# gMLP's v by seven products of halves instead of eight; the half-sums of its weight on GpSimd

## The chip, the cores and the metric

One core of a Trainium2 chip runs the whole program in one launch. The metric is the time of one execution on the device, in microseconds (us). A core has five engines that each work through an instruction list of their own, in order: TensorE (PE in the rows; its weight loads are PEld), VectorE (DVE), ScalarE (ACT), GpSimd (POOL) and SyncE (SP), whose list here issues nearly all transfers between DRAM and the on-chip memory. They wait for each other through semaphores.

## The reference

Batch 1, 512 tokens, width 1024, float32. A first block mixes three branches, then come a feed-forward part and a second block of two layers. What matters here, for h = rms_norm(x):

```
u, v, q, kv, nsa_g, xr, rg, mg = split(h @ w_in)
y_a = gelu(u) * (W_s @ layer_norm(gelu(v)) + b_s)     # gMLP: 4 chunks of 128 tokens, W_s lower triangular
y_b = nsa(q, kv, nsa_g, ...)                          # one of its parts: compress keys and values,
                                                      #   gelu((blocks + pe) @ w1) @ w2
y_c = rglru(xr, rg, ...)                              # the recurrent branch
merged = g0*(y_a @ w_br_a) + g1*(y_b @ w_br_b) + g2*(y_c @ w_br_c),   g = sigmoid(mg)
x = x + rms_norm(merged @ w_o); then the feed-forward part
```

v is 512 x 1024: h (512 x 1024) times w_v (1024 x 1024).

## The kernel before, in words

Numbers are held as two parts of lower precision, hi and lo (`split`, L140 to L150: ScalarE copies hi at L144, VectorE subtracts for lo at L145), and a product is three matmuls, hi*hi, hi*lo and lo*hi. A weight tile of 128x1024 is loaded raw by SP into `wr`, then split into `wh` and `wl` (`load_w`, L188). h lies on chip as `hT`, transposed, in both parts.

The program is written as Python generators that a clock of estimated times interleaves (`spawn`; `yield t` means "go on t us of matmul time later"); a scheduler then sets each engine's order from that and from priorities, where `load_w` is moved ahead. What results is a fixed list for each engine.

- Early, NSA's keys and values: `fold` (L1408 to L1413) copies a projection through SP into windows (`K2<-R`), `blocks` adds the position code (L1434), and the hidden layer of 16 weight tiles (nsa_wk1, then nsa_wv1, four raw tiles of 512 KB each) is followed by a gelu (L434 to L438), transposes of its result g on TensorE (L138) and the second layer. Between these, TensorE does products that are wanted later (`mgproj`, weight w_mg, L1384). The raw weights have two buffers here.
- Then the rest of NSA, the recurrent branch, and `br_b` for NSA's output.
- `gmlp` (L760): v by `T_` twice (L769 to L786), once for each half of v's columns: 96 matmuls of 128x512 each, tokens by columns. Each 128-token result goes through a gelu (ScalarE L434, L435, L437; VectorE L436, L438), its statistics (L777), and after the second half through the normalization (mean and variance L780, a small Newton iteration L154 to L166, L782). Then for each of 8 column blocks: u's block by `F_` and its gelu; `mixed` (L791), spawned with a delay of 12 for the first block and 4 for the others, which multiplies wT with all four normalized tiles vg; and `br_add` (L626 to L636), 24 matmuls with w_br_c, after which VectorE updates bT (L635) and the merged sum (L636).
- In the second block one product is already done by seven products: `TS_` computes the four quarter blocks of a product from seven products of half size, 24 matmuls each, with the weight's four half-sums taken from DRAM. `weight_sums` makes these: for a group it loads four 128x512 pieces q of the weight (L372), GpSimd subtracts four times in place (L375 to L378), SP stores four results (L381). Each of four q buffers exists once, so the next group's loads wait for the stores of the group before.

Of the kernel before, what the change touches and what calls it, by code (L numbers as in the profile page):

```python
# [7 lines left out]
F32 = mybir.dt.float32  # L8
# [3 lines left out]
ALU = mybir.AluOpType  # L12
# [38 lines left out]
class Block:  # L51
# [136 lines left out]
    def load_w(self, src, into=None):  # L188
        with self.tc.high_priority(offset=50):
            self.nr += 1  # L190
            rp, n = (self.rawp, 4) if self.rawp and self.nr % 3 else (self.wp, 2)
            raw = rp.tile([P, 1024], F32, tag="wr", name=self.nm("wr"), bufs=n)
            self.nc.sync.dma_start(out=raw, in_=src)
            if into is not None:
                self.split(*into, raw)
                return into
            self.nw += 1
            wp, n = (self.wx, 1) if self.wx and self.nw % 5 == 0 else (self.wp, 4)
            wh = wp.tile([P, 1024], F32R, tag="wh", name=self.nm("wh"), bufs=n)
# [278 lines left out]
    def block1(self):  # L478
        tc, nc, A = self.tc, self.nc, self.A
# [10 lines left out]
        self.nr, self.rawp = 0, None  # L490
# [49 lines left out]
        with tc.tile_pool(name="gmlp", bufs=1, side="right", reuse_waits="tile") as gp:  # L540
            ya = self.new_op(self.yp, "y", bufs=2)
            mT = self.gmlp(gp, ya, yc)
# [217 lines left out]
    def gmlp(self, gp, ya, yc):  # L760
# [12 lines left out]
        def done(half):  # L773
            def f(t, ps):
                o = slice(half * 512, half * 512 + 512)
                self.gelu(ps, gp, out=vg[t][:, o])
                v.bn_stats(st[t][:, half, :], vg[t][:, o])  # L777
                if half:
                    mv = self.sm(2)
                    v.bn_aggr(mv, st[t])  # L780
                    r = self.rsqrt(mv[:, 1:2])
                    v.tensor_scalar(vg[t], vg[t], mv[:, 0:1], r, op0=ALU.subtract, op1=ALU.mult)  # L782
            return f

        for half in range(2):
            self.T_(self.tok(self.hT), A["w_v"][half], 8, done(half), outer=2 + 2 * half)  # L786

        ps = self.pst()
# [32 lines left out]
    def ffn(self, hf, fp, es_w):  # L821
# [5 lines left out]
        def done(i, ps):  # L827
            if i == 0:
# [5 lines left out]
                self.w_sums = {}  # L834
# [535 lines left out]
    def nsa(self):  # L1370
# [27 lines left out]
        with tc.tile_pool(name="cmp", bufs=1, side="right", reuse_waits="tile") as cp:  # L1398
# [4 lines left out]
            k2s = []  # L1403

# [367 lines left out]
```

## Time and profile before

| | |
|---|---|
| median of three runs | 2508.74 us (2506.1 to 2509.05) |
| the profiled execution | 2508.13 us, its span 2506.3 us |
| busy: PE, DVE, ACT, POOL | 2483.5, 1469.9, 1081.4, 179.0 us |
| TensorE's granted clock, mean | 0.999 of full speed |
| chain of work that ended last, by engine | PE 89%, DVE 4%, ACT 3%, DMA 2% |
| TensorE's largest waits in the whole span | 2.7 us for wl (five times), 2.2 us for the first gain row |

The span is what the trace covers; the time lies 1.83 us above it. The profile's page gives the busy time of each engine and follows the chain of work back from the last instruction. A row of a timeline is start, duration, engine, line, operation, result<-operands; in brackets stands the idle time before it and what ended it. TensorE's matmuls overlap: one of 128x512 has a duration of 0.39 us, but starts come closer together.

### The profile page before, as it was taken

To read this page: it belongs to the slowest core of one execution; us is meant where nothing else is said; L and a number is where in the kernel's file an instruction comes from. 1 tells how busy PE (TensorE), PEld (TensorE's weight loads), DVE (VectorE), ACT (ScalarE), POOL (GpSimd) and SP (SyncE) were. 2 spreads that over 40 slices of the span, in tenths; PEclk is the share of its full clock that TensorE was granted. 3 is DMA by queue.
4 is the path that set the end of the run, shared out by engine and by line. 5 is a ranking of instruction groups with operands and counts; after the bars stand their busy time and mean duration, and the time that the engine had idled before them with its cause. 6 is when DMAs were issued, how large, how long until landed. Compare 5 with 4: busy or idle time off the path is not lost.

```text
span 2506.3 us, 31435 instructions
## 1 busy us (share of the span) xinstructions
PE 2483.5 (99%) x11802; PEld 2047.5 (82%) x11802; DVE 1469.9 (59%) x2719; ACT 1081.4 (43%) x1852; POOL 179.0 (7%) x152
## 2 busy tenths in 40 slices
PE   9999999999999999999999999999999999999998
PEld 7877777888888888888888788888888888888887
DVE  6567665776656787626633536765484343375635
ACT  4477666875334333324443532333253344223323
POOL 0023332000000110001100000003020000000000
PEclk9999999999999999999999999999999999999999
DMA  6522222223345886544432222226454222322233
GB/s 183 173 79 78 72 70 93 93 91 110 118 130 173 269 273 211 183 139 141 165 119 92 63 87 82 91 78 219 147 171 154 90 84 63 98 76 93 68 101 118
DMA packets 110074, 309.54 MB, mean 124 GB/s; under 512 B 14409, under 2 KB 20425, under 8 KB 109794
## 3 DMA queue, kind: packets, MB, share of 16 engines
q1 hardware_dynamic: 109200, 306.29, 38.1%
q8 instruction: 92, 1.51, 0.3%
q10 hardware_dynamic: 722, 1.25, 0.1%
q14 instruction: 60, 0.49, 0.1%
HBM read 273.84 MB, written 21.00 MB: 118 GB/s over the span
## 4 chain that ended last, share of the span: by engine, by line
PE 89%; DVE 4%; ACT 3%; DMA 2%; issue 1%; POOL 1%; SPq 0%; ACTq 0%; DVEq 0%; POOLq 0%
PE ps L129 86%; PE ps L138 3%; DVE wl L145 1%; DMA wr<-in_w_out_dram 1%; ACT S L1534 1%; ACT wh L144 1%; DMA wr<-in_w_o_dram 0%; DVE H L145 0%; DVE yr L145 0%; POOL X L1077 0%; DVE PTl L145 0%; DVE S L1528 0%; DMA wr<-in_w_v_dram 0%; POOL S L1541 0%; ACT S L1539 0%
## 5 line engine op out<-in xcount | busy, mean ns | idle before, releaser
L129 PE MATMUL ps<-h,wh 128*128 128x512 f32 (+1 forms) x4000 | 1244.4, 391 | 0.0
L129 PEld LDWEIGHTS ps<-h,wh 128*128 128x128 f32 x4000 | 734.7, 188 | 139.5 <-issue 5.1
L145 DVE TENSOR_TENSOR wl<-wr,wh 128x1024 fp32r<-128x1024 f32 x395 | 492.6, 1250 | 486.9 <-ACT wh L144 486.5
L129 PE MATMUL ps<-h,wl 128*128 128x512 f32 (+1 forms) x2000 | 774.0, 387 | 0.1
L144 ACT ACTIVATE wh<-wr 128x1024 fp32r<-128x1024 f32 x395 | 417.3, 1059 | 807.0 <-PE ps L129 627.9
L129 PEld LDWEIGHTS ps<-h,wl 128*128 128x128 f32 x2000 | 376.2, 188 | 75.4 <-DVE wl L145 0.5
L129 PE MATMUL ps<-wh,h 128*128 128x512 f32 x672 | 211.6, 392 | 0.0
L129 PEld LDWEIGHTS ps<-wh,h 128*128 128x128 f32 x672 | 126.3, 188 | 27.0 <-DVE h L145 0.8
L129 PE MATMUL ps<-wl,h 128*128 128x512 f32 x336 | 131.5, 391 | 0.9 <-DVE wl L145 0.9
L129 PE MATMUL ps<-y,wh 128*128 128x512 f32 x384 | 119.4, 391 | 0.0
L129 PE MATMUL ps<-wh,f 128*128 128x512 f32 x288 | 89.7, 390 | 0.0
L1541 POOL TENSOR_SCALAR S<-S,sm 128x128 f32<-128x128 f32 (+3 forms) x64 | 69.6, 1099 | 213.6 <-ACT Q L144 77.7
L129 PEld LDWEIGHTS ps<-y,wh 128*128 128x128 f32 x384 | 71.5, 188 | 14.3
L375 POOL TENSOR_TENSOR q<-q,q 128x512 f32<-128x512 f32 x8 | 11.8, 1474 | 950.9 <-DMA q<-in_w_va_dram 950.9
L129 PE MATMUL ps<-yr,wh 128*128 128x512 f32 x256 | 78.8, 389 | 0.0
L660 DVE SCALAR_TENSOR_TENSOR acc<-aw,cact,acc 128x512 f32<-128x512 f32 x96 | 75.7, 790 | 5.1 <-issue 2.3
L1534 ACT ACTIVATE S<-S,sm 128x128 f32<-128x128 f32 (+3 forms) x128 | 70.2, 550 | 19.1 <-DVE sm L1532 18.8
L145 DVE TENSOR_TENSOR PTl<-ps,PTh 128x512 fp32r<-128x512 f32 (+1 forms) x96 | 65.1, 684 | 22.5 <-ACT PTh L144 21.6
L144 ACT ACTIVATE PTh<-ps 128x512 fp32r<-128x512 f32 (+1 forms) x96 | 56.0, 588 | 49.1 <-PE ps L138 43.9
L1131 DVE CUSTOM_DVE_ANT_0 P<-ps,c_masks 128x128 f32<-128x128 f32 (+1 forms) x96 | 31.2, 325 | 76.3 <-PE ps L129 74.1
L129 PEld LDWEIGHTS ps<-wl,h 128*128 128x128 f32 x336 | 63.2, 188 | 14.5 <-DVE wl L145 1.9
L129 PE MATMUL ps<-y,wl 128*128 128x512 f32 x192 | 74.8, 390 | 0.0
(362 smaller groups left out, 3331.7 us busy)
## 6 DMA issues: line engine op xcount, KB each, us to landing
aw<-in_w_ada_dram SPq DMA_DIRECT2D x96, 256.0 KB, 4.3
wr<-in_w_qk_dram SPq DMA_DIRECT2D x48, 512.0 KB, 3.5
wr<-in_w_ffn_in_dram SPq DMA_DIRECT2D x44, 512.0 KB, 3.9
wr<-in_w_g_dram SPq DMA_DIRECT2D x32, 512.0 KB, 3.5
wr<-in_w_qr_dram SPq DMA_DIRECT2D x32, 512.0 KB, 3.4
wr<-in_w_mg_dram SPq DMA_DIRECT2D x24, 512.0 KB, 3.5
wr<-in_w_ffn_out_dram SPq DMA_DIRECT2D x22, 512.0 KB, 3.9
wr<-in_w_va_dram SPq DMA_DIRECT2D x20, 512.0 KB, 5.6
```

What stands on the lines that cost most here:

```text
L129: self.nc.tensor.matmul(out, a, b, start=start, stop=stop, skip_group_check=True)
L138: self.nc.tensor.transpose(out, in_, self.ident[:k, :k])
L144: nc.scalar.activation(hi, src, AF.Copy)
L145: nc.vector.tensor_sub(lo, src, hi.bitcast(F32))
L375: g.tensor_sub(b11, b12, b11)
L660: v.scalar_tensor_tensor(acc, w, self.cact[:, k:k + 1], acc, op0=ALU.mult, op1=ALU.add)
L1131: v.tensor_tensor_reduce(dst, pv, mask, 1.0, -3e38, ALU.add, ALU.max, mx[:, n:n + 1])
L1534: nc.scalar.activation(Ps[h], Ps[h], AF.Exp, scale=0.125, bias=nm_[:, h:h + 1], accum_out=ls[:, h:h + 1])
L1541: nc.gpsimd.tensor_scalar(Ps[h], Ps[h], r[:, h:h + 1], None, op0=ALU.mult)
```

## The change

v is computed by `TS_`: seven products of 24 matmuls in place of two `T_` of 96. Four half-sums of h are made first, in the four vg tiles: two additions on VectorE, two on GpSimd (L790), then three operations on VectorE (L791 to L794) and one on GpSimd (L795); they are split into a tile hs. Two results are kept in e (in `yt` buffers), others in the upper halves of vg; VectorE adds products up from PSUM (L345 to L361). The weight's half-sums come from DRAM (`w_sums["v", 0]`), where `weight_sums` puts them: it is spawned in NSA's compressed branch with paces 3.0, 6.5 and 2.5 and a delay of 6.0, and its q tiles lie in that branch's pool. During `TS_` two of four raw weight tiles go to the pool wx, and its wh and wl are not used for split weights. ya takes its buffer after `TS_`.

```diff
 load_w:
-            rp, n = (self.rawp, 4) if self.rawp and self.nr % 3 else (self.wp, 2)
+            rp, n, tag = (self.rawp, 4, "wr") if self.rawp and self.nr % 3 else (self.wp, 2, "wr")
+            if self.raws_in_wx and self.nr % 4 > 1:
+                rp, n, tag = self.wx, 1, "wh" if self.nr % 4 == 2 else "wl"
...
-            wp, n = (self.wx, 1) if self.wx and self.nw % 5 == 0 else (self.wp, 4)
+            wp, n = (self.wx, 1) if self.wx and not self.raws_in_wx and self.nw % 5 == 0 else (self.wp, 4)
 gmlp:
-        for half in range(2):
-            self.T_(self.tok(self.hT), A["w_v"][half], 8, done(half), outer=2 + 2 * half)
+        hs = self.new_op(self.yp, "y", bufs=2)
+        flat = lambda x, j: x[:, 2 * j:2 * j + 2, :].rearrange("p k q -> p (k q)")
+        a12, a21, a11, a22 = vg
+        for x, kh, th in ((a21, 0, 1), (a22, 1, 1), (a11, 0, 0), (a12, 1, 0)):
+            part = (slice(None), slice(4 * kh, 4 * kh + 4), slice(256 * th, 256 * th + 256))
+            (v if th else nc.gpsimd).tensor_add(x.rearrange("p (k q) -> p k q", k=4), self.hT.hi[part].bitcast(F32),
+                                                self.hT.lo[part].bitcast(F32))
+        v.tensor_add(a22, a21, a22)
+        v.tensor_sub(a21, a11, a21)
+        v.tensor_sub(a11, a22, a11)
+        nc.gpsimd.tensor_sub(a12, a12, a11)
+        for j, x in ((1, a11), (0, a22), (2, a21), (3, a12)):
+            self.split(flat(hs.hi, j), flat(hs.lo, j), x)
+        places = iter([gp.tile([P, S], F32, tag="yt", name=self.nm("e"), bufs=2) for _ in range(2)]
+                      + [vg[t][:, 512:] for t in range(4)])
+        self.raws_in_wx = True
+        self.TS_(self.hT, [A["w_v"][i] for i in range(2)], self.w_sums["v", 0],
+                 lambda j, k, t, lo: flat(hs.lo if lo else hs.hi, j)[:, k * 256 + t * P:k * 256 + t * P + P],
+                 lambda: next(places), done)
+        self.raws_in_wx = False
+        ya = self.new_op(self.yp, "y", bufs=2)
 nsa, compressed branch:
+            self.w_sums["v", 0] = self.dp.tile([8, P, D], F32, tag="v0", name="v0")
+            self.spawn(self.weight_sums([A["w_v"][i] for i in range(2)], self.w_sums["v", 0], cp, (3.0, 6.5, 2.5)), 6.0)
```

How the orders change, at the two places of which the prediction speaks. In the names a number behind a tile tells its use apart; lines after L372 are 1 to 20 higher in the changed program.

**The SP queue in the compressed branch.** Before, from the last load of nsa_wk1 on (wr are raw weights of 512 KB):

```order
L193 DMA wr_691<-in_nsa_wk_dram 128x1024
L193 DMA wr_733<-in_w_mg_dram 128x1024
L193 DMA wr_771<-in_nsa_wv_dram 128x1024
L193 DMA wr_794<-in_nsa_wv_dram 128x1024
L193 DMA wr_812<-in_nsa_wv_dram 128x1024
L193 DMA wr_830<-in_nsa_wv_dram 128x1024
L193 DMA wr_857<-in_w_mg_dram 128x1024
L193 DMA wr_913<-in_w_k_dram 128x1024
```

The changed order in the same place, from the load of w_mg on (q are the pieces of w_v that GpSimd works on, v_388 is the DRAM tile of its half-sums):

```order
L195 DMA wr_778<-in_w_mg_dram 128x1024
L195 DMA wr_820<-in_nsa_wv_dram 128x1024
L383 DMA v_388<-q_682 128x512
L383 DMA v_388<-q_686 128x512
L383 DMA v_388<-q_684 128x512
L383 DMA v_388<-q_688 128x512
L195 DMA wr_843<-in_nsa_wv_dram 128x1024
```

and six rows further on:

```order
L374 DMA q_864<-in_w_v_dram 128x512
L195 DMA wr_887<-in_nsa_wv_dram 128x1024
L383 DMA v_388<-q_858 128x512
L383 DMA v_388<-q_862 128x512
L383 DMA v_388<-q_860 128x512
L195 DMA wr_914<-in_w_mg_dram 128x1024
L383 DMA v_388<-q_864 128x512
L195 DMA wr_978<-in_w_k_dram 128x1024
```

The second load of nsa_wv1 has moved behind the four stores of one group, the next w_mg load behind three stores of the next.

**TensorE and VectorE at the first use of v.** TensorE before, the end of w_br_c's second product (ps_6373) with the first matmuls of wT and the normalized tiles vg between its own:

```order
L129 MATMUL ps_6373<-y_4644,wh_6369 128x512
L129 MATMUL ps_6373<-y_4645,wh_6369 128x512
L129 MATMUL ps_6373<-y_4644,wl_6370 128x512
L129 MATMUL ps_6383<-wT,vg_5844 128x128
L129 MATMUL ps_6383<-wT,vg_5845 128x128
L129 MATMUL ps_6383<-wT,vg_5846 128x128
L129 MATMUL ps_6383<-wT,vg_5847 128x128
L129 MATMUL ps_6373<-y_4644,wh_6369 128x512
L129 MATMUL ps_6373<-y_4645,wh_6369 128x512
```

TensorE in the changed order, the end of w_br_c's second product (ps_6486):

```order
L129 MATMUL ps_6486<-y_4709,wh_6482 128x512
L129 MATMUL ps_6486<-y_4710,wh_6482 128x512
L129 MATMUL ps_6486<-y_4709,wl_6483 128x512
L129 MATMUL ps_6496<-wT,vg_5907 128x128
L129 MATMUL ps_6514<-wT,vg_5907 128x128
L129 MATMUL ps_6543<-h_96,wh_6539 128x512
L129 MATMUL ps_6543<-h_97,wh_6539 128x512
L129 MATMUL ps_6543<-h_96,wl_6540 128x512
L129 MATMUL ps_6543<-h_96,wh_6539 128x512
```

VectorE in the changed order, from bT's update with ps_6486 on:

```order
L636 SCALAR_TENSOR_TENSOR bT_6478<-bT_6478,ps_6486 128x512
L162 SCALAR_TENSOR_TENSOR sm_6310<-sm_6307,sm_6304 128x1
L777 BN_STATS bn_5912<-vg_5908 128x6
L166 SCALAR_TENSOR_TENSOR sm_6311<-sm_6310,sm_6307 128x1
L637 TENSOR_TENSOR mg_777<-mg_777,bT_6478 128x512
L162 SCALAR_TENSOR_TENSOR sm_6314<-sm_6311,sm_6304 128x1
L780 BN_AGGR sm_6338<-bn_5912 128x2
L438 SCALAR_TENSOR_TENSOR g_6397<-g_6397,g_6396 128x512
L166 SCALAR_TENSOR_TENSOR sm_6315<-sm_6314,sm_6311 128x1
L145 TENSOR_TENSOR wl_6712<-wr_6709,wh_6711 128x1024
```

and on to the normalization (L782) of the tile vg_5907 that TensorE's next matmul wants:

```order
L162 SCALAR_TENSOR_TENSOR sm_6318<-sm_6315,sm_6304 128x1
L440 SCALAR_TENSOR_TENSOR g_6398<-g_6397,g_6396 128x512
L166 SCALAR_TENSOR_TENSOR sm_6319<-sm_6318,sm_6315 128x1
L154 TENSOR_SCALAR sm_6340<-sm_6338 128x1
L782 TENSOR_SCALAR vg_5907<-vg_5907,sm_6302,sm_6319 128x1024
```

Before, VectorE had v's four normalizations done ahead of that update; now the last two stand behind it, and the first matmul with wT has moved from between the next product's matmuls to right behind w_br_c's last.

## Rows read from the trace of the kernel before

**Rows 1.** The page's part 1: busy us, share of the span, instructions.
```profile
PE 2483.5 (99%) x11802; PEld 2047.5 (82%) x11802; DVE 1469.9 (59%) x2719; ACT 1081.4 (43%) x1852; POOL 179.0 (7%) x152
```

**Rows 2.** Windows: stretch, us, then busy time by engine; clock, DMA share, GB/s.
```profile
36.00:100.00 64.00, 62.19 (x332) 52.37 (x331) 36.17 (x43) 30.01 (x40) 0.25 (x2) 1.00 0.62 180
...
585.00:640.00 55.00, 55.00 (x243) 45.19 (x242) 39.83 (x84) 27.34 (x40) 0.00 (x0) 1.00 0.31 100
```

**Rows 3.** Timeline of PE from 583.9 us: start, us, operation (x2: two matmuls).
```profile
584.01 0.62 PE L129 MATMUL ps<-wh,h 128*128 128x512 f32 x2
...
584.69 0.62 PE L129 MATMUL ps<-wh,h 128*128 128x512 f32 x2
```

**Rows 4.** Tile q (weight sums of the second block): its transfers, both ways.
```profile
DMA to landing us min/median/max: 2.2/3.8/5.9
```

**Rows 5.** DMA issues, 815 to 1740 us: count, KB each, median us to landing.
```profile
va<-q SPq DMA_DIRECT2D x32, 256.0 KB, 3.8
...
wr<-in_w_va_dram SPq DMA_DIRECT2D x10, 512.0 KB, 6.2
```

**Rows 6.** Timeline of POOL, one group of four subtractions: start, us.
```profile
1718.96 1.29 POOL L375 TENSOR_TENSOR q<-q,q 128x512 f32<-128x512 f32 x1 [5.91 <-DMA q<-in_w_va_dram]
1720.33 2.15 POOL L376 TENSOR_TENSOR q<-q,q 128x512 f32<-128x512 f32 x1
...
1723.93 1.30 POOL L378 TENSOR_TENSOR q<-q,q 128x512 f32<-128x512 f32 x1
```

**Rows 7.** Timeline of the SP queue's issues, 60 to 90 us (x4: from first to last).
```profile
60.44 2.39 SPq L1413 DMA_DIRECT2D K<-R  x4
...
66.63 0.33 SPq L193 DMA_DIRECT2D wr<-in_w_mg_dram  x1
71.16 10.99 SPq L193 DMA_DIRECT2D wr<-in_nsa_wv_dram  x4
82.97 0.33 SPq L193 DMA_DIRECT2D wr<-in_w_mg_dram  x1
```

**Rows 8.** Timeline of ACT, 74 to 88 us: start, us, [idle before <- what ended it].
```profile
74.60 1.06 ACT L144 ACTIVATE wh<-wr 128x1024 fp32r<-128x1024 f32 x1 [3.06 <-DMA wr<-in_nsa_wv_dram]
...
77.90 0.41 ACT L437 ACTIVATE g<-g 128x256 f32<-128x256 f32 x1
...
87.42 1.06 ACT L144 ACTIVATE wh<-wr 128x1024 fp32r<-128x1024 f32 x1 [1.06 <-DMA wr<-in_w_mg_dram]
```

**Rows 9.** Timeline of PE, 80 to 90 us.
```profile
80.72 0.44 PE L138 MATMUL ps<-ident,g 128*128 128x128 f32 x2 [0.50 <-DVE g L438]
...
89.10 0.63 PE L129 MATMUL ps<-h,wh 128*128 128x512 f32 x2
```

**Rows 10.** Timelines of PE and DVE where T_ for gMLP's v begins.
```profile
578.80 0.39 PE L129 MATMUL ps<-wh,h 128*128 128x512 f32 x1
...
579.33 0.69 DVE L145 TENSOR_TENSOR y<-xc,y 128x512 fp32r<-128x512 f32 x1 [0.70 <-ACT y L144]
```

**Rows 11.** Timeline of DVE from 619 us: operations that follow each other without idle time.
```profile
619.22 0.68 DVE L436 SCALAR_TENSOR_TENSOR g<-g,g 128x512 f32<-128x512 f32 x1
619.83 1.22 DVE L145 TENSOR_TENSOR wl<-wr,wh 128x1024 fp32r<-128x1024 f32 x1
620.96 0.68 DVE L438 SCALAR_TENSOR_TENSOR vg<-g,g 128x512 f32<-128x512 f32 x1
```

**Rows 12.** Timeline of DVE, 1713 to 1720 us: the same split with POOL idle, then busy.
```profile
1713.54 1.23 DVE L145 TENSOR_TENSOR wl<-wr,wh 128x1024 fp32r<-128x1024 f32 x1 [1.64 <-ACT wh L144]
1718.97 2.36 DVE L145 TENSOR_TENSOR wl<-wr,wh 128x1024 fp32r<-128x1024 f32 x1 [4.21 <-ACT wh L144]
```

**Rows 13.** Timelines of DVE and PE: v's last normalization, its first use.
```profile
634.03 0.16 DVE L166 SCALAR_TENSOR_TENSOR sm<-sm,sm 128x1 f32<-128x1 f32 x1
634.23 0.81 DVE L782 TENSOR_SCALAR vg<-vg,sm,sm 128x1024 f32<-128x1024 f32 x1
...
641.58 1.05 PE L129 MATMUL ps<-wT,vg 128*128 128x128 f32 x8
```

More of the change, by code (lines that the diff above doesn't have):

```diff
@@ L190, in load_w @@
             self.nr += 1
-            rp, n = (self.rawp, 4) if self.rawp and self.nr % 3 else (self.wp, 2)
-            raw = rp.tile([P, 1024], F32, tag="wr", name=self.nm("wr"), bufs=n)
+            rp, n, tag = (self.rawp, 4, "wr") if self.rawp and self.nr % 3 else (self.wp, 2, "wr")
+            if self.raws_in_wx and self.nr % 4 > 1:
+                rp, n, tag = self.wx, 1, "wh" if self.nr % 4 == 2 else "wl"
+            raw = rp.tile([P, 1024], F32, tag=tag, name=self.nm("wr"), bufs=n)
             self.nc.sync.dma_start(out=raw, in_=src)
@@ L489, in block1 @@
         self.nw, self.wx = 0, None
-        self.nr, self.rawp = 0, None
+        self.nr, self.rawp, self.raws_in_wx, self.w_sums = 0, None, False, {}
         self.wp = op(self.es, "w")
@@ L540, in block1 @@
         with tc.tile_pool(name="gmlp", bufs=1, side="right", reuse_waits="tile") as gp:
-            ya = self.new_op(self.yp, "y", bufs=2)
-            mT = self.gmlp(gp, ya, yc)
+            mT = self.gmlp(gp, yc)
         es_m.close()
@@ L757, in rnn, with gmlp @@
         fill()
-    def gmlp(self, gp, ya, yc):
+    def gmlp(self, gp, yc):
         nc, A, v = self.nc, self.A, self.nc.vector
@@ L771, in gmlp @@
         st = [self.smp.tile([P, 2, 6], F32, tag="bn", name=self.nm("bn"), bufs=6) for _ in range(4)]
[L773 to L783, printed above, removed]
@@ L785, in gmlp, with done @@
-        for half in range(2):
-            self.T_(self.tok(self.hT), A["w_v"][half], 8, done(half), outer=2 + 2 * half)
+        def done(t, half, z):
+            o = slice(half * 512, half * 512 + 512)
+            self.gelu(z, gp, out=vg[t][:, o])
+            v.bn_stats(st[t][:, half, :], vg[t][:, o])
+            if half:
+                mv = self.sm(2)
+                v.bn_aggr(mv, st[t])
+                r = self.rsqrt(mv[:, 1:2])
+                v.tensor_scalar(vg[t], vg[t], mv[:, 0:1], r, op0=ALU.subtract, op1=ALU.mult)
@@ L833, in done @@
                 self.spawn(self.ada(pool[0], 1.2))
-                self.w_sums = {}
                 self.spawn(self.all_weight_sums(0, pool[0], (12.0, 16.0, 12.0)))
```

## The prediction, made before the changed kernel was run

> **What bounds the kernel now.** The page's first part comes first: TensorE (PE) is busy 99% of the span, VectorE (DVE) 59%, GpSimd (POOL) 7% [rows 1]. So an instruction off TensorE costs time only where TensorE waits for it, and a matmul that goes is worth its pitch. The windows of the two stretches the change touches say the same: from 585 to 640 us, where gMLP's v is computed, TensorE never stops, and from 36 to 100 us, the stretch of NSA's compressed branch, it stands for 1.8 us [rows 2]. I then read both programs' orders, queue by queue, looked for the rows on which TensorE waits in the changed one, and priced them from the rows below. Every engine and the SP queue (which issues the loads) works in order: what stands behind a waiting row waits too.
>
> The sum is made on the profiled execution, 2508.13 us. The median of the three runs, 2508.74 us, lies 0.6 us above it, which is less than anything said here. About 5 us (0.2%) is what a measurement of this kernel can tell from no change: the bounds are 2503.7 and 2513.8.
>
> **The change, part by part.**
>
> *24 matmuls less.* Two T_ of 96 become seven products of 24: 192 to 168. Three matmuls of 128x512 take from 584.01 to 584.69, 0.227 us each [rows 3]. 24 x 0.227 = **-5.45 us**, all of it on the path.
>
> *The weight's sums beside the compressed branch.* They add 32 transfers of 256 KB on the SP queue, among the loads that feed TensorE there, and 16 GpSimd subtractions. GpSimd did almost nothing in this stretch, so only the SP queue matters. Of the four groups the first two lie where SP stood still anyway (nothing of them is on the path). The last two I follow with the rows of the same code for the second block: a 256 KB load lands after 3.8 us [rows 4], a store after 3.8 us [rows 5], and the four subtractions take from 1718.96 to 1725.23, 6.3 us [rows 6].
> - The last K<-R copies are issued from 60.44 to 62.83 [rows 7]. Group 2's last stores follow them, some 0.4 us each, to about 63.8. Group 3's loads write the buffers those stores read, so the last waits till 63.8 + 3.8 = 67.6, and lands at 71.4. The subtractions start when the first two are there (about 70.5): the fourth ends at 76.8.
> - The four stores of group 3 now stand before the second load of wv. It is issued at about 77.2 and lands after 3.4 us (as the first one, issued at 71.16 and used at 74.60 [rows 7, 8]) to 6.2 us (a load beside much traffic [rows 5]): 80.6 to 83.4. On ScalarE its split (1.06) stands ahead of the gelu's tanh, which was done at 77.90 [rows 8]; then come the tanh (0.41) and 0.4 on VectorE, and TensorE's transposes of g start at 82.5 to 85.3, not at 80.72 [rows 9].
> - Group 4's loads wait for group 3's stores to land (77.2 + 3.8 = 81.0) and land at 84.8; the subtractions run from about 83.5. The next mg load stands behind the stores of the first three, so it is issued at about 88.8 instead of 82.97. Before, 4.45 us passed from that issue to its split at 87.42, and 1.68 from there to TensorE's first use at 89.10 [rows 7 to 9]. 88.8 + 4.45 + 1.68 = 94.9: **+5.8 us**. With a landing of 3.4 or 6.2 us it is 4.8 or 7.6. This holds the 1.8 to 4.6 us of the step before, since TensorE then only waits less here. Nothing gives it back: TensorE's order holds no other work there. The least is 0, if every landing is much quicker.
>
> One page of the Trainium skill would make this cheaper: "DMA: Bandwidth & Descriptors" (Anatomy of one DMA — SWDGE (gpsimd) path) fits 2.0 us plus bytes/436e3 for transfers that GpSimd issues, an estimated 2.6 us for 256 KB. The rows have 3.8 on SP's queue [rows 4, 5]. By the page the chain's four transfers would be 4.8 us shorter, this term about 1 us and the sum 2513.9. I go by the rows.
>
> *The opening of the seven products.* The half-sums of h need VectorE just when the first weights need their low parts (wl). VectorE is done with the recurrent branch at 579.33 + 0.61, TensorE begins at 578.80 [rows 10]. A 128x1024 operation holds VectorE for 1.13 us, a 128x512 one for 0.61 us [rows 11]. Ahead of the wl of the third product's second weights stand ten of the first and two of the second kind, 12.5 us; it ends at 593.6 and is wanted after 61 matmuls, at 592.65: 1.0 late. Of the next product's weights the first wl stands two splits further on, ends at 597.0 and is wanted after 73 matmuls, at 595.4: 1.6 late in all. The second of those splits waits for GpSimd's 128x1024 subtraction, which follows VectorE's at 591.3 and takes 2.6 to 4.3 us (twice its 128x512 rows, 1.29 in [rows 6] and up to 2.15 beside VectorE): with 1.06 on ScalarE and two operations on VectorE the wl ends at 597.2 to 598.9, up to 3.5 late. While GpSimd worked on two tensors, a wl took 2.36 us instead of 1.23 [rows 12]; of VectorE's operations here three lie beside GpSimd's, 3.4 us more at most. So 1.6 to 6.9; I take **+3.0**, nearer the low end, since GpSimd's two additions can start before VectorE's.
>
> The rule behind that last row is in "GPSIMD Engine Reference" (Specifications) of the Trainium skill: GpSimd shares its SBUF interfaces with VectorE, against instructions with two SBUF inputs. The trace agrees, with 2.36 us against 1.23. If the rule held for all 128x1024 operations here, the term would be 6.9 and the sum 2522.6.
>
> *The layer norm of v comes too late.* The largest term. Before, the last normalization of v (634.23 + 0.81) was done 6.5 us before TensorE's first matmul on it (641.58) [rows 13]. Seven products finish v's tiles nearly together at their end, and VectorE has some dozen more additions from PSUM and six more wl before it. In the changed order TensorE's very next row after the last matmul of w_br_c's second product is the matmul of wT with vg; on VectorE, bT's update, which waits for that last matmul, stands 14 rows ahead of the normalization of that vg. So whatever VectorE did before, TensorE stands while VectorE does five 128x512 operations (3.0 us), a wl (1.13), eight small ones (some 0.1 each; 0.16 alone) and the normalization (0.81) [rows 11, 13]: 5.8 us. Six matmuls later the next vg is wanted, and VectorE needs 3.2 us for it (two 128x512, eight small ones, 0.81) while TensorE has 1.8 us of work: 1.4 more. **+7.2 us**. The low end is 5.8; if VectorE comes to bT up to 2.3 us behind TensorE it is 9.5. It should be nearly level there: from the sixth product's first result VectorE has 27 operations of 128x512, seven wl, two normalizations and some 26 small ones up to bT, 29 us; TensorE has 127 matmuls, 28.8 us.
>
> *No cost.* The third and later splits of half-sums on ScalarE lie in its idle time; six more 512 KB loads at 0.33 us of SP each are covered, since SP is mostly idle beyond 100 us; w_sums' reads replace reads of w_v. If that cover fails it is a wl late by a landing, 3.4 us once.
>
> **Sum:** 2508.13 - 5.45 + 5.8 + 3.0 + 7.2 = **2518.7 us**.
>
> **The rivals.**
> 1. *Only the products count* (faster). The sums hide in SP's idle time and the normalization is done before TensorE asks. Then 2508.13 - 5.45 = 2502.7. For it: GpSimd and SP have much idle time. Against: the order of VectorE's rows around bT, which no duration can undo. It decides at TensorE's first wT matmul: this case needs it to start within 0.5 us of w_br_c's last.
> 2. *The compressed branch hides the sums, the rest is as forecast.* 2518.7 - 5.8 = 2512.9: not measurably slower, or just. Its condition is that each of the chain's four transfers is 1.4 us shorter than 3.8; the shortest of this kind took 2.2 [rows 4]. This is where the skill's page on DMA, above, would put it.
> 3. *Everything at its upper end*: 2508.13 - 5.45 + 7.6 + 6.9 + 9.5 = 2526.7. This is where GpSimd slows VectorE on every row they share and loads are slow beside the sums' traffic.
> 4. *The change does less than it says*: seven products that start late for want of weights, as half the raw loads go to other buffers. TensorE's order has 24 rows less, so the products are there; the first raw tile's buffer comes free 50 matmuls (11.4 us) ahead, where a landing of 3.4 and a split of 2.2 are needed. Only a landing beside heavy traffic, twice, would cost: 2518.7 + 2 x (6.2 - 3.4) = 2524.3.
>
> **How the numbers follow.** The forecast has 0.52, rival 1 0.05, rival 2 0.22, rival 3 0.14, rival 4 0.07. The range goes from 2507, which takes in rival 2 with the low ends of its terms (2508.13 - 5.45 + 0 + 0 + 5.8 = 2508.5), to 2530, above rivals 3 and 4. Faster has rival 1 and a little more: 0.06. Of rival 2, and of the forecast with low ends, 0.18 lies below 2513.8: same. Slower 0.76.
>
> **What would show it.** In the changed profile TensorE's list of waits has a new wait on VectorE's normalization (about 6 and then 1 us), waits on wl near the third and fourth product, and after 80 us longer waits for the transposes' g or the next mg's wl; the window from 36 to 100 us holds some 6 us less TensorE work. TensorE has 24 matmuls fewer. I am wrong if the wT matmul follows w_br_c's without a gap, or if the mg load is issued before 85 us.

## The result, and the profile after

The changed kernel takes **2530.75 us** (median of five runs, 2526.8 to 2533.52), the kernel before 2508.74 on the same chip: ratio 1.009, 95% interval 1.0079 to 1.0101, slower by 22 us. The forecast was 2518.7 in a range of 2507 to 2530: the sign is right, the size is half of what came, and the range ends 0.75 us too low. The profiled execution took 2533.52 us, the slowest of the five; its span is 2531.7.

TensorE has the 24 matmuls less, and VectorE, ScalarE and GpSimd have more to do (the page's part 1; before: [rows 1]):

```profile
PE 2490.3 (98%) x11778; PEld 2050.7 (81%) x11778; DVE 1499.4 (59%) x2746; ACT 1092.7 (43%) x1864; POOL 210.9 (8%) x171
```

Fewer matmuls with more busy time is the first hint: the matmuls themselves became slower. I cut the span at three instructions that both programs have: the first matmul of K with Q, at 121.58 us before; the first matmul for gMLP's v, at 578.80; and the first of the feed-forward part, at 808.42. That makes four stretches: NSA's compressed branch, attention and recurrent branch, gMLP, and the rest. After, they are 13.3, 0.2, 9.5 and 2.4 us longer, although gMLP holds 24 matmuls less. So both losses lie where the change works. The rest differs by -1.8 to +2.4 us between kernels that are the same there; the 2.4 of this execution hold two waits for a weight, 0.81 and 0.76 us at 2495.80 and 2497.06, and a granted clock of 0.50 from 2498 to 2500, which no other kernel has there. TensorE's waits in the whole span (line, what it waited for: total us, times, longest):

```profile
PE ps L129 <- DVE wl L145: 9.3, 10, 3.9
PE ps L129 <- DVE sm L156: 7.0, 1, 7.0
PE ps L129 <- ACT wh L144: 3.9, 3, 1.7
PE ps L138 <- DVE g L440: 3.0, 1, 3.0
```

Before, wl was waited for 2.7 us in all, and the other three together under 2 us. The windows (columns as in [rows 2], the first and third stretch answer to its rows) show what the waits did besides:

```profile
36.00:100.00 64.00, 55.74 (x276) 46.64 (x274) 36.71 (x39) 24.31 (x32) 18.10 (x14) 0.95 0.81 255
92.00:94.00 2.00, 2.00 (x11) 2.00 (x11) 1.69 (x2) 0.56 (x2) 1.92 (x2) 0.50 0.48 182
585.00:640.00 55.00, 51.14 (x216) 41.34 (x215) 48.46 (x56) 32.58 (x41) 5.52 (x1) 0.97 0.47 152
612.00:614.00 2.00, 1.06 (x3) 0.92 (x4) 2.00 (x3) 2.00 (x4) 0.00 (x0) 0.82 0.10 18
614.00:616.00 2.00, 2.00 (x6) 1.54 (x6) 2.00 (x4) 1.79 (x3) 0.00 (x0) 0.50 0.97 287
616.00:618.00 2.00, 2.00 (x9) 1.62 (x8) 1.49 (x2) 1.03 (x2) 0.00 (x0) 0.83 0.75 250
668.00:670.00 2.00, 2.00 (x8) 1.45 (x7) 1.26 (x4) 0.00 (x0) 0.00 (x0) 0.50 0.00 0
```

The seventh number is the clock granted to TensorE. It was 1.00 in both stretches before. Now, behind each longer wait, it is 0.50 for some microseconds: the lower of its two levels, 1.2 instead of 2.4 GHz. TensorE's timeline behind the wait in the opening of the seven products shows the price; compare the pitch with [rows 3]:

```profile
608.69 0.39 PE L129 MATMUL ps<-wh,y 128*128 128x512 f32 x1
612.93 0.53 PE L129 MATMUL ps<-wl,y 128*128 128x512 f32 x1 [3.86 <-DVE wl L145]
613.28 1.04 PE L129 MATMUL ps<-wh,y 128*128 128x512 f32 x2
614.11 0.63 PE L129 MATMUL ps<-wl,y 128*128 128x512 f32 x1
...
615.82 1.03 PE L129 MATMUL ps<-wh,y 128*128 128x512 f32 x2
616.67 0.41 PE L129 MATMUL ps<-wl,y 128*128 128x512 f32 x1
```

The eight matmuls from 613.28 to 616.67 take 3.39 us, 0.42 each; at 0.227 it would be 1.82. The wait of 3.86 us cost 1.6 us more than its length.

**The compressed branch.** The SP queue (before: [rows 7]):

```profile
68.50 2.70 SPq L374 DMA_DIRECT2D q<-in_w_v_dram  x4
71.26 0.42 SPq L195 DMA_DIRECT2D wr<-in_w_mg_dram  x1
75.70 0.33 SPq L195 DMA_DIRECT2D wr<-in_nsa_wv_dram  x1
76.85 5.24 SPq L383 DMA_DIRECT2D v<-q  x4
82.20 0.38 SPq L195 DMA_DIRECT2D wr<-in_nsa_wv_dram  x1
...
90.17 3.57 SPq L383 DMA_DIRECT2D v<-q  x3
94.02 0.33 SPq L195 DMA_DIRECT2D wr<-in_w_mg_dram  x1
```

The second load of wv stands behind four stores, and goes out at 82.20, the mg load at 94.02 instead of 82.97. An earlier mg load is late too: it stands behind the third group's loads and goes out at 71.26 instead of 66.63. TensorE pays (its rows with more than 1 us of idle time from 36 us to this stretch's end; before: [rows 9]):

```profile
78.69 0.73 PE L129 MATMUL ps<-h,wh 128*128 128x512 f32 x2 [1.39 <-ACT wh L144]
80.66 0.69 PE L129 MATMUL ps<-h,wl 128*128 128x512 f32 x1 [1.24 <-DVE wl L145]
90.48 0.44 PE L138 MATMUL ps<-ident,g 128*128 128x128 f32 x2 [2.95 <-DVE g L440]
100.32 0.73 PE L129 MATMUL ps<-h,wh 128*128 128x512 f32 x2 [1.69 <-ACT wh L144]
```

The first two are the product with the weight of that earlier mg load. ScalarE's split of it stood until the load landed (ScalarE's timeline):

```profile
77.58 1.06 ACT L144 ACTIVATE wh<-wr 128x1024 fp32r<-128x1024 f32 x1 [2.68 <-DMA wr<-in_w_mg_dram]
```

**The normalization of v.** VectorE, then TensorE (before: [rows 13]); the third block is before's TensorE row behind the eight matmuls of wT in those rows:

```profile
660.11 0.68 DVE L636 SCALAR_TENSOR_TENSOR bT<-bT,ps 128x512 f32<-128x512 f32 x1
...
665.03 0.81 DVE L782 TENSOR_SCALAR vg<-vg,sm,sm 128x1024 f32<-128x1024 f32 x1
```

```profile
665.99 1.20 PE L129 MATMUL ps<-wT,vg 128*128 128x128 f32 x4 [6.99 <-DVE sm L156]
666.84 1.20 PE L129 MATMUL ps<-h,wh 128*128 128x512 f32 x2
...
669.55 2.35 PE L129 MATMUL ps<-wT,vg 128*128 128x128 f32 x12
671.65 0.72 PE L129 MATMUL ps<-h,wh 128*128 128x512 f32 x2
```

```profile
642.38 0.71 PE L129 MATMUL ps<-y,wh 128*128 128x512 f32 x2
```

It is the row that the forecast named: bT's update 14 rows ahead of the normalization, TensorE idle over all of them, and for 1.1 us before, since VectorE came to the update that much behind TensorE's last matmul.

### The profile page after: what moved, and what is told of

Its sections match the earlier page's. It is cut to its first block, busy times and chain, and to the rows that moved or that the text cites. A ratio compares the mean times of both kernels' runs of the same rounds, so it can differ in the third digit from the quotient of the medians.

```text
span 2531.7 us, 31526 instructions
## 1 busy us (share of the span) xinstructions
PE 2490.3 (98%) x11778; PEld 2050.7 (81%) x11778; DVE 1499.4 (59%) x2746; ACT 1092.7 (43%) x1864; POOL 210.9 (8%) x171
## 4 chain that ended last, share of the span: by engine, by line
PE 85%; DVE 6%; ACT 3%; DMA 3%; issue 1%; POOL 1%; SPq 0%; ACTq 0%; POOLq 0%; DVEq 0%
PE ps L129 82%; PE ps L138 3%; DVE wl L145 2%; DMA wr<-in_w_out_dram 1%; ACT S L1554 1%; ACT wh L144 1%; DMA wr<-in_w_o_dram 0%; DMA wr<-in_w_mg_dram 0%; DVE H L145 0%; SPq L1433 0%; DVE yr L145 0%; DVE PTl L145 0%; DVE S L1548 0%; DVE xc L712 0%; DVE lr L689 0%
## 5 line engine op out<-in xcount | busy, mean ns | idle before, releaser
L145 DVE TENSOR_TENSOR wl<-wr,wh 128x1024 fp32r<-128x1024 f32 x401 | 501.5, 1254 | 485.2 <-ACT wh L144 484.6
L144 ACT ACTIVATE wh<-wr 128x1024 fp32r<-128x1024 f32 x401 | 423.2, 1058 | 805.3 <-PE ps L129 610.7
L129 PE MATMUL ps<-wh,h 128*128 128x512 f32 x592 | 187.7, 394 | 0.3 <-ACT h L144 0.3
L129 PEld LDWEIGHTS ps<-wh,h 128*128 128x128 f32 x592 | 111.6, 189 | 24.3 <-DVE h L145 0.8
L129 PE MATMUL ps<-wl,h 128*128 128x512 f32 x296 | 116.1, 392 | 0.9 <-DVE wl L145 0.9
L377 POOL TENSOR_TENSOR q<-q,q 128x512 f32<-128x512 f32 x12 | 18.1, 1512 | 863.7 <-DVE sm L164 485.1
L129 PEld LDWEIGHTS ps<-wl,h 128*128 128x128 f32 x296 | 56.0, 189 | 13.3 <-DVE wl L145 2.0
```

The source lines that it names most:

```text
L129: self.nc.tensor.matmul(out, a, b, start=start, stop=stop, skip_group_check=True)
L144: nc.scalar.activation(hi, src, AF.Copy)
L145: nc.vector.tensor_sub(lo, src, hi.bitcast(F32))
L377: g.tensor_sub(b11, b12, b11)
```

## The experiments

The theory after the result: the forecast's three waits are there and of about the forecast's size; the rest is TensorE's clock behind them. If so, each wait that is cured gives back more than its length. The rivals: the traffic of the sums slows everything, or VectorE's and GpSimd's added work does. The first kernels undo one part each, the later ones look for a place where the sums cost nothing. All results first; the last four columns are the four stretches defined above, against before's, in us, from each profiled execution.

| kernel | median us | ratio, 95% interval | compressed | attention, recurrent | gMLP | rest |
|---|---|---|---|---|---|---|
| the change | 2530.75 | 1.0090, 1.0079 to 1.0101 | +13.3 | +0.2 | +9.5 | +2.4 |
| e1 sums only | 2520.38 | 1.0049, 1.0036 to 1.0061 | +13.9 | 0.0 | -0.6 | -0.5 |
| e2 sums in recurrent branch | 2538.48 | 1.0122, 1.0108 to 1.0136 | +0.6 | +14.6 | +7.3 | +7.3 |
| e3 a split later | 2529.31 | 1.0084, 1.0070 to 1.0097 | +17.7 | +0.1 | +5.0 | -1.8 |
| e4 first use of v later | 2525.23 | 1.0071, 1.0057 to 1.0085 | +15.4 | 0.0 | +0.9 | 0.0 |
| e5 GpSimd's queue | 2530.39 | 1.0089, 1.0075 to 1.0103 | +13.3 | +0.2 | +11.9 | +0.4 |
| e6 a half-sum on VectorE | 2527.04 | 1.0079, 1.0065 to 1.0093 | +12.7 | +0.1 | +6.6 | -0.5 |
| e7 e4, e5 and e6 | 2519.64 | 1.0051, 1.0038 to 1.0063 | +11.7 | -0.4 | -1.5 | +0.9 |
| e8 sums in attention | 2529.97 | 1.0085, 1.0071 to 1.0099 | +0.5 | +11.1 | +8.6 | +0.8 |
| e9 transfers alone | 2513.09 | 1.0017, 1.0008 to 1.0026 | +7.9 | -0.1 | -0.9 | +0.5 |
| e10 e8, e4, splits later | 2519.52 | 1.0040, 1.0028 to 1.0053 | +0.8 | +11.5 | -3.5 | +0.3 |
| e11 sums 60 us later | 2514.86 | 1.0026, 1.0016 to 1.0035 | +0.8 | +8.2 | -2.4 | +0.6 |
| e12 fourth group at 423 us | 2505.94 | 0.9990, 0.9981 to 0.9999 | +1.1 | -0.2 | -2.4 | +0.9 |
| e13 fourth group at 343 us | **2506.19** | 0.9993, 0.9984 to 1.0002 | +1.1 | +1.1 | **-2.5** | -1.5 |

The stretches are of one execution each. The code of the compressed branch is the same in the change, e3, e4 and e6, and shows +12.7 to +17.7; that of gMLP is the same in the change, e5 and e8, and shows +8.6 to +11.9. By its time, the theory of the run came true in e1, e6, e12 and e13, the rival in e3, e5, e7, e8, e10 and e11; e2 is slower than both had it, e4 and e9 lie between. The stretches say which part of each theory failed.

**e1: the sums without the seven products** (before's kernel, with the change's line in the compressed branch).

```diff
+            self.w_sums["v", 0] = self.dp.tile([8, P, D], F32, tag="v0", name="v0")
+            self.spawn(self.weight_sums([A["w_v"][i] for i in range(2)], self.w_sums["v", 0], cp, (3.0, 6.5, 2.5)), 6.0)
```

> The kernel before (v by two T_, 192 matmuls) with the weight's half-sums made in the compressed branch and read by nothing. Theory (loads behind the sums' stores on the SP queue stop TensorE there, whatever is done with the sums): TensorE's transposes of g near 90.5 us as in the changed kernel and 13 us in all, 2508.7 + 13 = about 2522. Rival (the sums hide, the loss belongs to gMLP): about 2509, transposes near 81 us.

12 us slower with not one matmul less. The losses of the change split cleanly: 13 to 14 us belong to the sums in their place, the 9.5 to gMLP.

**e9: the same without GpSimd's subtractions.** The sums of the second block's second layer lose theirs too, which is outside the stretch.

```diff
-                g.tensor_sub(b11, b12, b11)
...
+                if pace[0] > 10:
+                    g.tensor_sub(b11, b12, b11)
...
```

> The kernel before with the sums' 32 transfers in the compressed branch, but without GpSimd's subtractions (the pieces are copied from w_v to DRAM, and nothing reads them). Same traffic as with the sums alone (2520.4, 12.5 us above the kernel before), no stores that wait for GpSimd. Theory (it is the chain load, 6.3 us of subtractions, store, load in front of the weights): two groups' subtractions, 12 us, leave the chain, and at most 4 us are lost, 2512 or less. Rival (the 8 MB of traffic is what delays the weights): 2518 or more.

The loss falls from 13.9 to 7.9 us in that stretch, with one wait over 1 us left from 36 us on (2.35). This execution was the slowest of eleven, though: by the medians the loss falls from 12.5 to 5.2 us. So the traffic and the stores ahead of the loads make about half of it (0.42 by the medians, 0.57 by the stretches). The other half goes with GpSimd's subtractions: the time they add to the chain load, subtract, store, and what they cost VectorE beside them (in the change a wl at 78.67 took 1.94 us, before 1.2). This run doesn't separate the two.

**e5: the sums' transfers on GpSimd's queue.** GpSimd's clearing of R goes to VectorE; the second layer's second sums go to that queue as well.

```diff
+        dma = (self.nc.sync if pace[0] > 10 else g).dma_start
...
-                    self.nc.sync.dma_start(out=q[-1], in_=src[half][c][:, o])
+                    dma(out=q[-1], in_=src[half][c][:, o])
```

> The changed kernel with the sums' transfers issued by GpSimd itself instead of SP (and the small memset of fold on VectorE, so that nothing of the branch waits for GpSimd). The traffic and the subtractions are the same. Theory (the order on SP's queue is what stops the loads): w_mg and nsa_wv are issued as in the kernel before, and most of the 13.3 us up to the first K,Q matmul goes: 2530.75 - 10 = about 2520. Rival (the traffic delays the loads): less than 3 us of it goes, 2528 or more.

Not a microsecond gained: 13.3 again. Freed from the SP queue, the sums' loads start while the kernel's first weights come in, whose issues are then 3.5 and 5.3 us later, and the waits have moved forward. TensorE's largest one:

```profile
75.76 1.12 PE L138 MATMUL ps<-ident,g 128*128 128x128 f32 x4 [7.09 <-ACT g L1439]
```

The order of the queue was one way of losing the time, not the cause by itself: in either order this stretch lost 13 us to the sums and their 8 MB (16 pieces in, 16 out, 256 KB each).

**e2: the sums in the recurrent branch**, their pieces in the spare weight buffers of wx.

```diff
-            self.spawn(self.weight_sums(..., cp, (3.0, 6.5, 2.5)), 6.0)
+            self.sums_in_wx = True
+            self.spawn(self.weight_sums(..., None, (6.0, 10.0, 6.0)), 6.0)
```

> The changed kernel with the sums moved out of the compressed branch into the recurrent one (their pieces in the two tiles of the pool wx, which the split weights give up there). Theory: the 13.3 us that the changed kernel had lost when the seven products began come back, 2530.75 - 13.3 = 2517.5, transposes near 81 us; up to 2522 if the fifth weight buffer was needed. Rival (the sums cost the same wherever they stand, by traffic): about 2530.

The first stretch is whole again (+0.6), and as much is lost where the sums are now, +14.6: four waits of TensorE over 1 us sum to 9.1, and (1 - granted clock) adds up to 5.1. (The flag of the edit also keeps later split weights out of wx, to which I put the +7.3 in the rest; no run tests that.) On SP three stores wait for their subtractions with a weight of xr behind them (SP's timeline):

```profile
451.68 5.43 SPq L388 DMA_DIRECT2D v<-q  x3
457.20 0.39 SPq L195 DMA_DIRECT2D wr<-in_w_xr_dram  x1
```

TensorE's largest wait of the stretch has another cause. GpSimd's four subtractions of a group run from 479 to 487 us, and beside them three of VectorE's operations, in front of the row that TensorE wants, take 1.72 to 1.75 us; in the kernel before they take 0.68 to 0.74. That is 3.1 of the 4.61 us (TensorE; one of the three; the same one before):

```profile
486.56 1.10 PE L129 MATMUL ps<-xh,gh 128*128 128x512 f32 x2 [4.61 <-ACT xh L144]
```

```profile
482.42 1.74 DVE L758 TENSOR_TENSOR xc<-xc,g 128x512 f32<-128x512 f32 x1
```

```profile
473.08 0.68 DVE L748 TENSOR_TENSOR xc<-xc,g 128x512 f32<-128x512 f32 x1
```

So in this place the rival that GpSimd's added work slows VectorE is true in part.

**e4: the normalization ahead of its use.** `mixed` is spawned with longer delays, so that TensorE has other products to do first, and the gelu's buffers are three.

```diff
-            yield 12.0 if c == 0 else 4.0
+            yield (26.0, 18.0, 12.0, 6.0, 4.0, 4.0, 4.0, 4.0)[c]
```

> The changed kernel with the first products of wT and v put later in TensorE's order (delays 26, 18, 12 and 6 for the first four column blocks, a third buffer for u's gelu). Theory: TensorE has u's third block to do while VectorE normalizes; the wait of 7.0 us goes, and with it some 2.7 us at half clock: 2530.75 - 9.6 = about 2521. Rival (VectorE's amount of work is the bound, not the order): the wait returns at the later place, 2528 or more.

The wait of 6.99 is gone, one of 1.50 at the third product is new, and gMLP falls from +9.5 to +0.9: 8.6 us for 5.5 us of waiting. Against e8 and e5, whose gMLP is the change's, it is 7.7 us for 5.9 and 11.0 for 6.1. That more comes back than the waits' length, each time, is the theory's main evidence. The medians lie only 5.5 us apart, not the 9.6 expected: the change's profiled execution was its slowest, and e4's compressed branch lost 2.1 us more.

**e3: the fourth half-sum split after the fifth product began; e6: that half-sum on VectorE.** In e3 the split reads its tile after part of it has been overwritten, so v is another one.

```diff
e3:
-        for j, x in ((1, a11), (0, a22), (2, a21), (3, a12)):
+        for j, x in ((1, a11), (0, a22), (2, a21)):
...
+        late = lambda: self.split(flat(hs.hi, 3), flat(hs.lo, 3), a12)
e6:
-        nc.gpsimd.tensor_sub(a12, a12, a11)
+        v.tensor_sub(a12, a12, a11)
```

> The changed kernel with the split of the fourth half-sum of h (the one GpSimd makes) written after the fifth product instead of ahead of the fourth. Theory: the wl of the fourth product no longer stands behind it on VectorE; the wait of 3.9 us at 612.9 goes, and with it the 1.7 us that the matmuls after it lost at half clock: 2530.75 - 5.5 = 2525.2. Rival (VectorE is behind anyway and the same time is lost at the normalization): 2530.

> The changed kernel with the fourth half-sum of h made by VectorE instead of GpSimd (1.1 us in place of 5.5 us). Theory (that GpSimd subtraction is what the split and the wl behind it waited for): the wait at 612.9 falls from 3.9 to at most 1 us, with the half-clock stretch behind it, 2530.75 - 4.5 = about 2526. Rival (VectorE's one operation more makes it later): 2530 or more.

Both take the wait of 3.86 away. As the wait of the normalization grew, to 9.24 and 7.81, and e6 has a new one of 1.46 at the third product, each has 1.6 us of waiting less in all; gMLP gains 4.5 and 2.9 us (3.6 and 2.0 against e8, the least of the change's gMLP). Again more comes back than the length of the waits. In e3 this hardly shows in the time, since its compressed branch lost 4.4 us more than the change's.

**e7: e4, e5 and e6 together.**

> The changed kernel with the three edits together: transfers of the sums on GpSimd's queue, the fourth half-sum on VectorE, the first products of wT later. Theory (three separate causes, and what is left is 24 matmuls less): from the seven products to the end 3 to 5 us less than in the kernel before, in the compressed branch 0 to 4 us more; 2508 - 4 + 2 = 2506, no more than 2510. Rival (the causes are one lack of VectorE or DMA capacity that moves on): 2515 or more.

The time is the rival's, but not by its reason: gMLP is 1.5 us faster than before's, and what is left is the compressed branch, where the part from e5 gave 1.6 us at most.

**e8: the sums in the attention stretch**, in four mg tiles that are free there. **e10: e8 with e4 and three of the four splits later.**

```diff
+        mgs = [self.mp.tile([P, S], F32, tag="mg", name=self.nm("mg"), bufs=8) for _ in range(8)]
...
+            self.spawn(self.weight_sums(..., mgs[4:], (9.0, 12.0, 6.0)), 10.0)
```

> The changed kernel with the sums moved to NSA's attention stretch, their pieces in the four mg tiles that are not yet in use there (the eight mg tiles are allocated ahead). Theory (the sums cost where TensorE's weights come just in time, and nothing where the loads run ahead): first K,Q matmul as in the kernel before (121.6), at most 3 us lost up to the recurrent branch, 2530.75 - 13.3 + (0 to 3) = 2517 to 2521. Rival (they cost some 13 us wherever they stand, as in the recurrent branch): 2530.

> The changed kernel with the sums in the attention stretch, the first products of wT later, and three of the four splits of h's half-sums written after the third and fourth product (the tiles dealt out so that nothing is overwritten early). Theory (what is left is 24 matmuls less): 2508 - 5.45, with 0 to 3 us for the sums and at most 2 at the third product: 2503 to 2508. Rival (VectorE's additional work turns up at another wait): 2512 or more.

The loss moved once more: 11 us in attention, most of it at these two of e8's TensorE rows (6.3 us) and in the slower clock behind them (3.4). In e10 gMLP itself is now 3.5 us faster than before's.

```profile
126.18 0.44 PE L129 MATMUL ps<-K,Q 128*128 128x128 f32 x2 [2.95 <-DVE sm L1551]
146.92 1.27 PE L138 MATMUL ps<-ident,S 128*128 128x128 f32 x4 [3.39 <-POOL S L1564]
```

**e11: the sums 60 us later**, started from the list of projections; mg's last ones come after the others.

```diff
-            seq += take(2) + [(mgproj, 4), (qproj, 6), (qproj, 7)] + take(4) + [(mgproj, 5), (mgproj, 6)] + take(16)
+            seq += take(2) + [(qproj, 6), (qproj, 7)] + take(1) + [(sums, ())] + take(16) + [(mgproj, 4), (mgproj, 5), (mgproj, 6)]
```

> The changed kernel with all cures of e10_all_moved in the gMLP stretch (normalization ahead of the matmuls of wT, the splits of three half-sums later), and the sums of w_v again in the attention stretch, in the four tiles of mg that stand free there, but 60 us later: at about 178 to 212 us instead of 119 to 160, where the first K and Q copies and the first S rows of GpSimd stand in before. The last four projections of mg come after the other fillers, so that the four tiles are free. If the 11.0 us that e8_sums_in_attention and the 11.6 that e10_all_moved lost in that stretch came from the collision with the first copies and S rows, this placement loses 0 to 3 us there, the gMLP stretch keeps its 3.2 us and the sum is 2505.5 to 2508.5 (ratio 0.999 to 1.000). If GpSimd's four subtractions in a chain (5.2 us, in front of rows on which TensorE's transposes wait) or the traffic cost the same wherever they stand, it loses 8 to 12 us again and the sum is 2514 to 2518 (ratio 1.002 to 1.004).

8.2 us are lost, which is the rival's number, but at one place. Beside three of the four groups TensorE waits no longer than 0.4 us. Beside the fourth, GpSimd waited for its loads with S rows behind it (GpSimd's timeline), TensorE for those S rows (its own), and the clock fell (window):

```profile
217.92 1.27 POOL L388 TENSOR_TENSOR mg<-mg,mg 128x512 f32<-128x512 f32 x1 [5.15 <-DMA mg<-in_w_v_dram]
...
223.31 1.83 POOL L1578 TENSOR_SCALAR S<-S,sm 128x256 f32<-128x256 f32 x2
```

```profile
224.29 0.69 PE L138 MATMUL ps<-ident,S 128*128 128x128 f32 x2 [6.35 <-POOL S L1578]
```

```profile
228.00:230.00 2.00, 2.00 (x7) 1.71 (x6) 1.85 (x5) 0.00 (x0) 0.00 (x0) 0.50 0.18 47
```

**e12 and e13: the fourth group elsewhere.** In e12 other paces move it behind the last S rows; there two of mg's projections are written into the group's tiles between its loads and its subtractions, so these sums and projections come out changed. In e13 a projection of mg goes through the first tile and holds the group's load back, mg's last projections wait for the sums, and the paces are 4, 6 and 2. The other three groups' subtractions begin within 2.5 us of e11's in both.

```diff
e12:
-            (9.0, 12.0, 6.0)
+            (12.0, 16.0, 6.0)
e13:
+            T = mgs[4] if AHEAD.index(i) == 9 else np_.tile([P, S], F32, tag="ma", name=self.nm("ma"), bufs=2)
...
+                summing.append(self.spawn(self.weight_sums(..., mgs[4:], (4.0, 6.0, 2.0), groups)))
...
+ take(1) + [(sums, (0, 1, 2))] + take(9 - 5) + [(sums, (3,))] + take(16) + [(lambda: self.wait(*summing), ()), ...
```

> e11_sums_late with other paces (12, 16, 6 instead of 9, 12, 6), by which GpSimd's subtractions of the fourth group come after its last S rows, in the gap that before shows at 413 to 433 us, instead of at 217.9, where GpSimd waited 5.15 us for the group's loads with an S row behind it and TensorE then waited 6.35 us for that row. If that one in-order wait and the lower clock behind it made e11's loss in the attention stretch (9.0 us), the stretch now loses 0 to 3 us, and the sum is 2505 to 2508.5 (ratio 0.9985 to 1.0005): the first version not slower than before. If the loss is spread over the four groups and their traffic, it stays at 2512 to 2515 (ratio 1.0015 to 1.003), and a wait shows beside another group or where ScalarE writes mg behind the last stores.

> e11_sums_late with the fourth group of sums held back: one of the projections of mg that are stored to DRAM (the tenth) goes through the first of the four tiles, and the fourth group's first load stands behind its store, so that GpSimd's four subtractions come at about 340 us, after the S rows of a unit and in front of a gap of 8.9 us that before shows there; the other three groups stay at 180 to 212 us. The last four projections of mg wait until the sums are done. If the one in-order wait at 217.9 us was e11's loss in the attention stretch, the stretch loses 0 to 2 us, the gMLP stretch ends 1 to 3 us earlier than before's, and the sum is 2505 to 2508.5 (ratio 0.9985 to 1.0005). If the chain of GpSimd's subtractions costs TensorE a wait wherever it stands, a wait of over 1 us shows behind 340 us, and the sum is 2510 to 2515 (ratio 1.001 to 1.003).

Both are level with before or 2 us faster (e12, which computes something else, by its interval 0 to 5 us), as the theory of the one wait had it. The same four subtractions and the same traffic, 205 or 125 us later, cost 1 us or nothing. In e13 nothing of the computation is left out, and gMLP is 2.5 us shorter than before's, of the 5.45 that the 24 matmuls are worth. Its largest wait there is in the opening, with the clock around it:

```profile
599.86 0.73 PE L129 MATMUL ps<-wh,y 128*128 128x512 f32 x2 [1.88 <-DVE y L145]
```

```profile
598.00:600.00 2.00, 0.14 (x1) 0.14 (x2) 2.00 (x3) 2.00 (x3) 0.00 (x0) 1.00 0.01 2
600.00:602.00 2.00, 2.00 (x9) 1.66 (x10) 2.00 (x3) 2.00 (x4) 0.00 (x0) 1.00 0.10 14
```

The interval of e13 holds 1.0: a gain of 2 us is not shown. What is shown is that the change's loss of 22 us can be had back without giving up the seven products.

## Why the prediction was right, and where it was wrong

- *The products, -5.45 us.* Right as far as it can be seen: 24 matmuls less, and gMLP faster by 3.5 and 2.5 us in e10 and e13, where waits of 1.9 us and some small ones are left in the opening.
- *The compressed branch, +5.8, at most 7.6: 13.3 measured.* The mechanism was right where it was followed, wv behind a group's stores, mg behind the next. The waits of this stretch sum to 8.8 us, against 1.76 before: 7.0 more, inside the bounds, but not for the forecast's reasons alone. The first two groups were put at nothing; the mg load behind the second's stores and the third's loads (71.26, not 66.63) made the waits of 1.39 and 1.24. And the dates were off: the last K<-R copies began at 63.70, not 60.44, and the second group's last stores ended at 67.96, not 63.8, so that the later mg load went out at 94.02, not 88.8. A 256 KB store landed after 3.2 us (median in this stretch, 3.8 assumed), a 512 KB load of wv after 5.6 (3.4 to 6.2 assumed): the small transfers were quicker than assumed, the weights' loads near their slow end. The other 6.3 us are not more waiting. Adding up (1 - granted clock) over the windows of 2 us from 80 to 106 gives 5.1; the hidden layer's first matmul came 1.7 us late.
- *The rule on transfers.* "DMA: Bandwidth & Descriptors" of the Trainium skill (Anatomy of one DMA — SWDGE (gpsimd) path) would have 2.6 us for 256 KB, an estimate from its fit for transfers that GpSimd issues; this stretch's 3.2 on SP's queue lies as far above it as below my 3.8. It would have made the term 1 us, and the waits alone were 7.
- *The opening, +3.0 (1.6 to 6.9): a wait of 3.86.* Right in place (the fourth product's first wl) and cause (e6 takes it away). GpSimd's last subtraction was slower than its bound, though, and VectorE beside it was not slowed at all. The two timelines, GpSimd's and VectorE's:

```profile
579.46 5.21 POOL L790 TENSOR_TENSOR vg<-h,h 128x1024 f32<-128x1024 f32 x2 [130.41 <-DVE g L440]
603.88 5.52 POOL L795 TENSOR_TENSOR vg<-vg,vg 128x1024 f32<-128x1024 f32 x1 [19.21 <-DVE vg L794]
```

```profile
603.66 1.21 DVE L145 TENSOR_TENSOR y<-vg,y 128x1024 fp32r<-128x1024 f32 x1
...
605.93 1.21 DVE L145 TENSOR_TENSOR y<-vg,y 128x1024 fp32r<-128x1024 f32 x1
```

  The forecast bounded the subtraction at 2.6 to 4.3 us; it took 5.52, twice the 2.6 of each addition. "GPSIMD Engine Reference" of the Trainium skill (Specifications) says that the two share their SBUF interfaces. The trace agrees, with 5.52 us against 2.6, but here GpSimd paid, where in [rows 12] and in e2 VectorE did.
- *The normalization, +7.2: a wait of 6.99.* The place and the rows between are right: from bT's update to the end of the normalization VectorE took 5.7 us, 5.8 forecast. That the sums are so near is luck: the 6.99 hold 1.1 us by which VectorE was behind, put at nothing, and the second wait (1.4) did not come, since the matmuls in front of the next vg ran at the lower clock and VectorE was ready in time. (Its 3.2 us for that vg do not follow from its prices: two at 0.61, eight at 0.1 and 0.81 are 2.8, and the wait 1.0.)
- **The step that failed** is the sum itself: it priced each wait at its length, and took what TensorE does afterwards at the pitch of [rows 3]. It had no term for the granted clock, since before's was 1.00 on every row that I read. From rows of after: 5.1 us in the compressed branch (above), 1.6 behind the wait in the opening, and about 2.7 behind the normalization's (six matmuls from 666.84 to 669.55 in 2.71 us instead of 1.36, and sixteen of wT, in two parts, in 2.95 instead of 1.6: before, eight took from 641.58 to 642.38). That closes gMLP's account: -5.45 + 3.86 + 6.99 + 1.6 + 2.7 = 9.7, and 9.5 was measured. With these 9.4 us more the forecast would have been 2528.1; larger waits and the late start in the compressed branch (1.2 and 1.7), the opening's 0.9 and the 2.4 us in the rest lead to 2534, against the profiled execution's 2533.5. That the clock makes the loss is read from windows, pitches and this account; no run held these same waits and took the fall of the clock away. Rows of e2 come near to it. Behind its gMLP a wait for wl of 2.00 us left the clock at 1.00 (and so did one of 2.30), and the nine matmuls from 1229.28 to 1231.34 kept their pitch, 0.23 us each; such a wait costs its length alone:

```profile
1228.94 0.50 PE L129 MATMUL ps<-wl,h 128*128 128x512 f32 x1 [2.00 <-DVE wl L145]
1229.28 0.62 PE L129 MATMUL ps<-wh,h 128*128 128x512 f32 x2
...
1231.34 0.62 PE L129 MATMUL ps<-wh,h 128*128 128x512 f32 x2
```

```profile
1228.00:1230.00 2.00, 1.06 (x5) 0.88 (x6) 2.00 (x2) 2.00 (x4) 2.00 (x1) 1.00 0.11 18
```

- *The rule on the clock.* "TensorE: Matmul & The Clock Gate" of the Trainium skill (HAM oscillation — how this bites in real kernels) says that idle gaps between bursts of matmuls put TensorE back to the lower clock. The traces agree: 0.50 behind the waits of 3.86 and 6.99 us. It should have been weighed beside the forecast's 5.8 us wait.
- *The rivals.* The three waits at their upper ends (2526.7) came nearest, for another reason: none of them was at its upper end. That only the products count fell with the wait of 6.99, that the compressed branch hides the sums with e1.

## What to carry to other kernels

Where TensorE is 99% busy, work that is "free" on an idle engine costs what stands behind it in the in-order lists of that engine and of its queue; find the place where nothing urgent stands behind it before pricing the gain. A wait of some microseconds on TensorE can cost its length and then a stretch of matmuls at half clock: here 1.6 us more behind one of 3.86 and 2.7 behind one of 6.99, and nothing behind one of 2.00. And a change that loses may be right in its core: the same seven products were 22 us slower or level, by the place of some small subtractions and of one normalization.

## What the runs showed that was not expected

- The clock did not fall behind every wait. It stayed at 1.00 around those of 0.88 (before), 1.88 (e13), 2.00 and 2.30 us (e2). It fell to 0.50 behind two of 0.81 and 0.76 us close together (after, at 2496 us), two of 1.39 and 1.24 us with 0.6 us of matmuls between (after, at 80 us), and behind those of 2.35 (e9), 2.95, 3.86 and 6.99 us. A wait's own length does not decide it; what does is left open.
- Which of GpSimd and VectorE pays for work beside each other varies. GpSimd's 128x1024 operation on two tensors took 2.6 us with VectorE idle for most of it, and 5.52 beside VectorE's run of two-tensor operations, which kept their 1.21 to 1.22 us. In e13 it took 4.38, and one of VectorE's splits beside it 2.83; in e2 GpSimd's 128x512 operation took 1.6 instead of 1.3, and VectorE's 1.74 instead of 0.68.
- The same 32 transfers and 16 subtractions cost 13.9, 14.6, 11.1, 8.2 and 1.1 us in five places (the stretch of e1, e2, e8, e11 and e13, one execution each).
